# Weight sums of a seven-product FFN moved from VectorE to adding DMA transfers in DRAM

## The chip, the cores and the metric

The kernel runs on one core of a Trainium2 chip. Its engines work from queues of their own and meet through semaphores: TensorE (PE: matmuls; PEld: its weight loads), VectorE (DVE), ScalarE (ACT), GpSimd (POOL) and SyncE (SP). SP only issues DMA transfers here; POOL issues a few and does small elementwise work; 16 DMA engines move the bytes of all queues. The metric is the device time of one execution in microseconds, as the median of several runs. In the profile L12 is line 12 of the kernel's file.

## The reference

One transformer layer on 512 tokens of width 1024, in float32, batch 1:

```
mod = silu(c) @ w_ada + b_ada                    # 9 rows: shift, scale, gate, three times
u = rms_norm(x) * (1 + sc1) + sh1
x = x + 0.5 * g1 * swiglu(u, ffn1_w_in, ffn1_w_out)
z = (rms_norm(x) * (1 + sc2) + sh2) @ w_mix + b_mix
y_a = sigmoid(o) * rms_norm(mlstm(conv(q, k), v, i, f))     # 4 heads
y_b = forgetting_attention(q, k, v, f)                      # 16 heads
x = x + g2 * ((sigmoid(g_a) * (y_a @ w_a) + sigmoid(g_b) * (y_b @ w_b)) @ w_out)
u = rms_norm(x) * (1 + sc3) + sh3
x = x + 0.5 * g3 * swiglu(u, ffn2_w_in, ffn2_w_out)

swiglu(u, w_in, w_out):  a, b = split(u @ w_in);  return (silu(a) * b) @ w_out
```

The hidden width of both FFNs is 2816, which is 22 blocks of 128. The change concerns the last product, h @ ffn2_w_out, with h = silu(a) * b.

## The kernel before, in words

**Precision.** Every float32 operand of a product is split into a high part (a copy rounded to float32r by ScalarE, L89) and a low part (the difference, by VectorE, L91), and each product is three matmuls (L108 to L110). A weight tile of 128 x 1024 arrives through SP into one of three buffers `raw` and is split into one of four pairs `wh`, `wl`; 24 matmuls use it.

**Stages.** In order of time: start and first FFN (to about 395 us of the span), the second norm, q and k with their convolution (to 467), four mLSTM heads whose weights W are built from a bias tile (to 550), 16 attention heads (to about 850), the two branches and the output projection (to about 1000), the third norm, the second FFN's input products (to about 1210), and its output products (to the end).

**The mLSTM heads.** `mlstm_w(h)` loads a row into all partitions (`Mb`, through SP), POOL adds a mask to it (`Mm`, L837), ScalarE takes exponentials of `Mm` and `Mb` into `W` (L850, L852), TensorE forms q k in four banks t, and VectorE multiplies the banks into `W` (L854), which empties them. `Mm`, `Mb` and the head's results share four buffers. The masks are made by POOL just before the first head (L1182, L1183). `fox_t` prepares attention heads in pairs; for the first two pairs POOL clears tiles `klz` (L946). POOL's next work after these is the addition of the two branches (L1253).

**The second FFN's output in seven products.** The 22 blocks of h make 11 pairs, the tokens are taken in two halves of 256 and the columns of ffn2_w_out in two halves of 512. A pair is then a product of 2 x 2 blocks, which is done with seven block products (Winograd's form) in place of eight. That needs sums on both sides:

- of h, in `pair_h`: for the pair's blocks E (even) and Ra (odd), VectorE forms four combinations while the second FFN's input products run (L384 to L389);
- of the weights, in `pair_weights`: with a0, a1 the column halves of the pair's even rows and b0, b1 those of its odd rows, it makes a1-a0, b0-b1+a1-a0, b1-a1+a0 and b1-a1. Each half of a pair's columns is loaded to SBUF by two transfers of 256 KB (L427), summed there by four VectorE operations of 128 x 256 (L434 to L437), and stored to a DRAM tile `ws` of 1 MB per pair by a transfer of 512 KB (L439). It is a generator: `ffn_in` steps it twice per block of h.

`pair_out` loads the sums from `ws` as further weight tiles and adds up the seven products: first P1, X and Y over all pairs, whose combinations U2 and U4 serve both token halves, then four more products, whose banks are added to x with the right signs at the end (`add`, L503 and L505).

**What sets the order.** The program is written as if sequential. A planner lays the instructions onto the engines' queues by its own costs: an instruction may be laid as soon as its operands are ready in the plan, and among ready ones the one written first goes first. On the chip each queue runs strictly in the planned order, and an instruction that waits holds those behind it. `issue_after(i)` ties what is written under it behind instruction i on the same queue, without a wait for i to end. Waits for data are put in by the framework. In the old version the loads of the sums are tied behind the last weight load, and the sums behind the last product of h.

Of the kernel before, what the change touches and what calls it, by code (L numbers as in the profile page):

```python
# [11 lines left out]
F32 = mybir.dt.float32  # L12
# [3 lines left out]
ALU = mybir.AluOpType  # L16
# [30 lines left out]
class Layer:  # L47
# [309 lines left out]

    def pair_h(self, ps_a, ps_b, j, c0, c1, hp, tp):  # L360


        nc = self.nc
        i, w, h0 = j // 2, c1 - c0, c0 // 256
        nh = w // 256
        s = self.tmp(tp, "sl")
        nc.scalar.activation(s[:, :w], ps_a[:, c0:c1], AF.Silu)
        hv = lambda t: t.rearrange("p (h t) -> p h t", t=256)
        if j % 2 == 0:
            if h0 == 0:  # L370
# [12 lines left out]
        A1 = self.A1[i] = hp.tile([P, 6, 256], F32R, name=self.nm("A1"), tag=f"A{i}", bufs=1)  # L383
        V(E[:, 1, :], E[:, 3, :], Ra[:, 1, :], op=ADD)  # L384
        V(E[:, 2, :], E[:, 1, :], E[:, 0, :], op=SUB)
        nc.scalar.activation(A1[:, 0:3, :], E[:, 0:3, :], AF.Copy)
        V(A1[:, 3:6, :], E[:, 0:3, :], A1[:, 0:3, :], op=SUB)
        V(Rb[:, 0, :], E[:, 0, :], E[:, 3, :], op=SUB)
        V(Rb[:, 1, :], Ra[:, 0, :], E[:, 2, :], op=SUB)  # L389

    def pair_rest(self, i, hp, dt):
# [17 lines left out]
            nc.vector.tensor_tensor(lo[n], R, hi, op=SUB)  # L409
        self.A2[i] = A2, *lo  # L410

    def pair_weights(self, w, hp, tp):


        nc = self.nc
        V = nc.vector.tensor_tensor
        NP = NJ // 2
        self.ws = [self.dp.tile([P, 4, 512], F32, name=self.nm("ws")) for i in range(NP)]
        ts = {}
        def load(u):  # L420
            i, c = u // 2, slice(u % 2 * 256, u % 2 * 256 + 256)

            t = ts[u] = hp.tile([P, 5, 256], F32, name=self.nm("s"), tag=f"A{NP - 1}", bufs=1) if u % 2 else                 tp.tile([P, 5, 256], F32, name=self.nm("s"), tag="st", bufs=1)
            for n in range(2):
                r = (2 * i + n) * P
                with self.tc.issue_after(self.last_raw.ins):
                    nc.sync.dma_start(t[:, 2 * n:2 * n + 2, :], w[r:r + P, :].rearrange("p (h n) -> p h n", h=2)[:, :, c])  # L427
        def sums(u):

            t = ts[u]  # L430
            s = lambda n: t[:, n, :]

            with self.tc.issue_after(self.last_mul.ins):
                V(s(4), s(3), s(1), op=SUB)  # L434
                V(s(1), s(1), s(0), op=SUB)
                V(s(3), s(3), s(1), op=SUB)
                V(s(2), s(2), s(3), op=SUB)  # L437
        def store(u):
            nc.sync.dma_start(self.ws[u // 2][:, :, u % 2 * 256:u % 2 * 256 + 256], ts.pop(u)[:, 1:5, :])  # L439
        for h in range(3 * NP + 1):  # L440
            m, r = h // 3, h % 3
            for u, n in ((2 * m, r), (2 * m + 1, r - 1), (2 * m - 1, r + 2)):
                if 0 <= u < 2 * NP and 0 <= n < 3:
                    (load, sums, store)[n](u)
            yield

    def pair_out(self, w, v, hp, tp, x_src):
# [32 lines left out]
        for tb in range(2):  # L480
            nc.scalar.activation(P1[tb], Z[tb], AF.Copy)
        for tb in range(2):
            V(U2[tb], X[tb], P1[tb], op=ADD)
        for tb in range(2):
            V(U4[tb], Y[tb], U2[tb], op=ADD)
        self.pair_split(NP - 1, hp, tp)
# [11 lines left out]
        g = [new("gb") for _ in range(2)]  # L498
        for h in range(2):
            nc.sync.dma_start(g[h], self.mod_d[v:v + 1, h * 512:(h + 1) * 512].to_broadcast([P, 512]))  # L500
        def add(src, half, tbs):
            t = self.tmp(tp, "rs")
            nc.vector.scalar_tensor_tensor(t, src, 0.5, g[half], op0=MUL, op1=MUL)  # L503
            for tb in tbs:
                V(self.x[tb][half], self.x[tb][half], t, op=ADD)  # L505
        def store(tb, half):
            nc.sync.dma_start(self.out[0, tb * P:(tb + 1) * P, half * 512:(half + 1) * 512], self.x[tb][half])
        tail = 2
        for i in range(NP - tail):
            o = prepare(i)  # L510
            for n in ("WZXY" if i == 0 else "ZYXW"):
                for tb in range(2):
                    step(n, tb, i, o)
            if i == 4:
                self.x_tiles()
                x_src()
            if i in (6, 7):
                tb = i - 6
                add(P1[tb], 0, (tb,))
                add(U2[tb], 0, (tb + 2,))  # L520
                add(U4[tb], 1, (tb, tb + 2))
        os = [prepare(i) for i in range(NP - tail, NP)]
        for n in "ZYXW":
            for tb in range(2):
                for i, o in enumerate(os):
                    step(n, tb, NP - tail + i, o)
                ps = banks[n][tb]
                if n == "Z":
                    add(ps, 0, (tb,))
                    store(tb, 0)  # L530
                elif n == "Y":
                    add(ps, 1, (tb,))
                    store(tb, 1)
                elif n == "X":
                    add(ps, 1, (tb + 2,))
                    store(tb + 2, 1)
                    add(ps, 0, (tb + 2,))
                else:
                    add(ps, 0, (tb + 2,))
                    store(tb + 2, 0)  # L540
# [568 lines left out]
    def run(self):  # L1109
# [67 lines left out]
        with tc.tile_pool(name="att", bufs=1) as ip:  # L1177
            self.maskM = ip.tile([P, P], F32, name="maskM")
            self.maskF = ip.tile([P, P], F32, name="maskF")
            for t, fill, sgn in ((self.maskM, BIG, 1), (self.maskF, -BIG, -1)):  # L1180

                nc.gpsimd.memset(t, 0.0)  # L1182
                nc.gpsimd.affine_select(t, t, pattern=[[sgn, P]], compare_op=ALU.is_ge, fill=fill,  # L1183
                                        base=0, channel_multiplier=-sgn)
            self.onz = ip.tile([P, NT, 2], F32, name="onz")
            nc.gpsimd.memset(self.onz[:, :, 0:1], 1.0)
# [19 lines left out]
            for h0, n, fill in ((0, 3, with_gates(self.v_mlstm(1, ip, ip), 1)), (2, 4, with_gates(self.fox_qkv(0, ip), 1))):  # L1206
                for f, h in ((self.mlstm_w, h0), (self.mlstm_w, h0 + 1), (self.mlstm_h, h0), (self.mlstm_h, h0 + 1)):
                    f(h, ip)
                    advance(fill, n)
                    if f == self.mlstm_h and h == 2:  # L1210
                        self.fox_t(0, yp)
                advance(fill, 99)
            for n in range(18):
                if n % 4 == 0 and n < 16:
                    advance(fill, 99)
                    g = n // 4
                    fill = with_gates(self.fox_qkv(g + 1, ip), 4) if g < 3 else (s for m in range(NK) for s in self.y_a(m, yp, ip))
# [56 lines left out]
        with tc.tile_pool(name="f2t", bufs=1) as tp, tc.tile_pool(name="f2h", bufs=1) as hp:  # L1274
# [1 line left out]
                self.dump(f"u3_{k}", self.uh[k].bitcast(F32))  # L1276
            x_spill(1)
            self.ffn_in_halves(A["ffn2_w_in"][0], 2, hp, tp)
            pw = self.pair_weights(A["ffn2_w_out"][0], hp, tp)
            step = lambda *_: next(pw, None)  # L1280
            self.ffn_in(A["ffn2_w_in"][0], 2, hp, tp, step, step)
            for _ in pw:
                pass
            self.pair_out(A["ffn2_w_out"][0], 8, hp, tp, lambda: self.x_load(self.x3_d))


# [28 lines left out]
```

## Time and profile before

| | us |
|---|---|
| median of 3 runs | 1354.39 |
| lowest and highest | 1353.95, 1356.48 |
| the profiled execution | 1354.64 |
| its span, first to last instruction | 1352.9 |
| granted TensorE clock | 0.999 |

The page gives the busy time of each engine as a share of the span, the chain of work that ended last with its shares by engine, and groups of equal instructions (line, engine, operation, written tile <- read tiles, shapes, count, then busy us and mean ns of one, then the idle time of the engine just before them). The timeline lists instructions with start and duration in us, and in brackets the idle time before one and what ended it. A row of a tile's view gives the shortest, median and longest duration in ns and the first and last start. Rows of transfers end with the KB of one and, for POOL's queue, the median us from issue to landing. The lines themselves stand in the prediction, beside the sentences that use them.

### The profile page before, as it was taken

What the parts mean: (1) busy time and instruction counts of PE and PEld (TensorE: products, weight loads), DVE (VectorE), ACT (ScalarE), POOL (GpSimd) and SP (SyncE); (2) the same over time, 40 slices, a digit from 0 to 9 for tenths busy, and PEclk for the clock granted to TensorE, in tenths of its full rate; (3) what the DMA queues carried; (4) which work ended last, traced back from release to release, by engine and by line L of the source; (5) the groups of instructions that cost most, each with busy time, mean ns of one, the idle gap of its engine ahead of it and who ended that gap; (6) DMA issues with size and microseconds to landing.
All of it is one profiled execution on the core that took longest, in us unless ns stands there. A gap on an engine that the chain in (4) does not pass through costs nothing.

```text
span 1352.9 us, 17800 instructions
## 1 busy us (share of the span) xinstructions
PE 1328.6 (98%) x6520; PEld 1113.0 (82%) x6520; DVE 887.8 (66%) x1661; ACT 589.4 (44%) x978; POOL 46.0 (3%) x71
## 2 busy tenths in 40 slices
PE   7999999999999999999999999999999999999997
PEld 6788887887888888988888888888788888888886
DVE  6866666655558767987686876446475655545776
ACT  4532333322235755556565676333353222223642
POOL 2000000000011101000000000002010000000000
PEclk9999999999999999999999999999999999999999
DMA  9676556665634434444243442354436677763474
GB/s 290 187 225 187 179 178 212 218 201 183 200 86 105 129 91 126 116 131 121 74 140 86 113 141 78 110 183 159 140 110 183 212 232 219 228 189 139 171 247 166
DMA packets 245691, 219.30 MB, mean 162 GB/s; under 512 B 12706, under 2 KB 206914, under 8 KB 245604
## 3 DMA queue, kind: packets, MB, share of 16 engines
q1 hardware_dynamic: 245124, 218.09, 52.9%
q8 instruction: 51, 0.84, 0.2%
q14 instruction: 36, 0.29, 0.1%
q0 software_dynamic: 416, 0.06, 0.0%
q10 hardware_dynamic: 64, 0.02, 0.0%
HBM read 194.47 MB, written 23.66 MB: 161 GB/s over the span
## 4 chain that ended last, share of the span: by engine, by line
PE 86%; DVE 7%; ACT 3%; DMA 2%; issue 1%; SPq 0%; DVEq 0%; ACTq 0%
PE g L110 22%; PE g L108 22%; PE g L109 22%; PE t L110 4%; PE t L108 4%; PE t L109 4%; PE g L697 2%; PE t L1041 2%; PE t L1011 1%; DVE wl L91 1%; PE t L982 1%; PE t L983 1%; PE t L697 1%; DVE fq L961 1%; DMA h_d<-hn 1%
## 5 line engine op out<-in xcount | busy, mean ns | idle before, releaser
L89 ACT ACTIVATE wh<-raw 128x1024 fp32r<-128x1024 f32 x236 | 244.2, 1040 | 434.1 <-PE g L109 143.4
L91 DVE TENSOR_TENSOR wl<-raw,wh 128x1024 fp32r<-128x1024 f32 x236 | 290.0, 1231 | 188.2 <-ACT wh L89 168.6
L108 PE MATMUL g<-uh,wh 128*128 128x512 f32 (+2 forms) x984 | 370.6, 377 | 0.8 <-ACT wh L89 0.7
L110 PE MATMUL g<-uh,wl 128*128 128x512 f32 (+2 forms) x984 | 369.6, 376 | 1.0 <-DVE wl L91 1.0
L109 PE MATMUL g<-ul,wh 128*128 128x512 f32 (+2 forms) x984 | 369.6, 376 | 0.0
L110 PEld LDWEIGHTS g<-uh,wl 128*128 128x128 f32 (+1 forms) x984 | 184.7, 188 | 35.7 <-DVE wl L91 1.8
L108 PEld LDWEIGHTS g<-uh,wh 128*128 128x128 f32 (+1 forms) x984 | 184.8, 188 | 34.5 <-ACT wh L89 1.4
L109 PEld LDWEIGHTS g<-ul,wh 128*128 128x128 f32 (+1 forms) x984 | 184.9, 188 | 33.2
L108 PE MATMUL g<-wh,uh 128*128 128x512 f32 (+1 forms) x320 | 111.9, 350 | 0.0
L110 PE MATMUL g<-wh,ul 128*128 128x512 f32 (+1 forms) x320 | 111.1, 347 | 0.0
L109 PE MATMUL g<-wl,uh 128*128 128x512 f32 (+1 forms) x320 | 110.9, 347 | 0.0
L284 DVE SCALAR_TENSOR_TENSOR acc<-raw,ccol,acc 128x1024 f32<-128x1024 f32 x49 | 62.8, 1282 | 13.0 <-DMA raw<-in_w_ada_dram 12.1
L108 PEld LDWEIGHTS g<-wh,uh 128*128 128x128 f32 x320 | 60.5, 189 | 7.8 <-DVE tk L896 0.5
L110 PEld LDWEIGHTS g<-wh,ul 128*128 128x128 f32 x320 | 60.5, 189 | 7.7
L109 PEld LDWEIGHTS g<-wl,uh 128*128 128x128 f32 x320 | 60.5, 189 | 7.4
L108 PE MATMUL g<-yh,wh 128*128 128x512 f32 x128 | 50.4, 394 | 0.0
L110 PE MATMUL g<-yh,wl 128*128 128x512 f32 x128 | 50.2, 392 | 0.0
L109 PE MATMUL g<-yl,wh 128*128 128x512 f32 x128 | 49.7, 388 | 0.0
L993 ACT ACTIVATE S<-S,mn 128x128 f32<-128x128 f32 (+1 forms) x64 | 35.6, 557 | 18.5 <-DVE mn L985 9.5
L108 PE MATMUL g<-wh,hh 128*128 128x512 f32 x88 | 35.0, 398 | 0.0
L110 PE MATMUL g<-wh,hl 128*128 128x512 f32 x88 | 34.9, 396 | 0.0
L108 PE MATMUL t<-wh,hh 128*128 128x512 f32 x88 | 34.8, 396 | 0.0
(319 smaller groups left out, 2054.8 us busy)
## 6 DMA issues: line engine op xcount, KB each, us to landing
raw<-in_ffn_w_in_dram SPq DMA_DIRECT2D x82, 512.0 KB
raw<-in_w_ada_dram SPq DMA_DIRECT2D x56, 512.0 KB
raw<-in_w_mix_dram SPq DMA_DIRECT2D x48, 512.0 KB
raw<-in_ffn_w_out_dram SPq DMA_DIRECT2D x33, 512.0 KB
s<-in_ffn_w_out_dram SPq DMA_DIRECT2D x44, 256.0 KB
ws<-s SPq DMA_DIRECT2D x22, 512.0 KB
ar<-in_w_ada_dram SPq DMA_DIRECT2D x32, 256.0 KB
raw<-in_w_mix_dram SPq DMA_DIRECT2D x32, 256.0 KB
```

The lines of the kernel that those rows point to most:

```text
L89: nc.scalar.activation(hi, src, AF.Copy)
L91: nc.vector.tensor_tensor(lo, src, hi, op=SUB)
L108: mm(ps, lh, rh, start=start, stop=False)
L109: mm(ps, lh, rl, start=False, stop=False)
L110: self.last_mm = mm(ps, ll, rh, start=False, stop=stop)
L284: nc.vector.scalar_tensor_tensor(acc, r, self.ccol[:, k:k + 1], acc, op0=MUL, op1=ADD)
L697: mm = nc.tensor.matmul(acc_ps[b], (wl if p == 1 else wh)[:, b % 2, s], self.ul[k] if p == 2 else self.uh[k], start=k == 0 and p == 0, sto ...
L961: nc.vector.scalar_tensor_tensor(lo, b[own, :], gc[own, :], d[own, :], op0=MUL, op1=SUB)
L982: nc.tensor.matmul(ps[:, :w], q[:, s], k[:, :w], start=True, stop=False)
L983: nc.tensor.matmul(ps[:, :w], q[:, s], kl[:, :w], start=False, stop=True)
L993: nc.scalar.activation(S[:, ws], S[:, ws], AF.Exp, scale=-1.0, bias=m, accum_out=sm[:, qb:qb + 1])
L1041: nc.tensor.matmul(po[:, q0:], vt[:, kb, i, :], Px[:, o:o + T - q0], start=n == 1, stop=n == 8)
```

## The change

The sums of the weights no longer pass through SBUF. For each pair three transfers copy a0, the two halves (b0, b1) and again b1 from ffn2_w_out into `ws`, DRAM to DRAM; four transfers that add to their target then make a0+a1, b1+a1, b0+(the first) and b0+b1+a0+a1. All 77 are issued on POOL's queue, tied behind the second mask's instruction (`mask`); the generator is stepped in the loop over the attention heads, and a pair's copies are written one step ahead of its sums. Since such a transfer only adds, the sums have other signs than before (a0+a1 in place of a1-a0 and so on), and the sums of h, U2 and the last additions to x change sign to match. The loads, VectorE sums and stores beside the second FFN's input products are gone.

```diff
     def pair_h(self, ps_a, ps_b, j, c0, c1, hp, tp):
...
-        V(E[:, 1, :], E[:, 3, :], Ra[:, 1, :], op=ADD)
-        V(E[:, 2, :], E[:, 1, :], E[:, 0, :], op=SUB)
+        V(E[:, 1, :], E[:, 3, :], Ra[:, 1, :], op=SUB)
+        V(E[:, 2, :], E[:, 0, :], E[:, 1, :], op=SUB)
         nc.scalar.activation(A1[:, 0:3, :], E[:, 0:3, :], AF.Copy)
         V(A1[:, 3:6, :], E[:, 0:3, :], A1[:, 0:3, :], op=SUB)
-        V(Rb[:, 0, :], E[:, 0, :], E[:, 3, :], op=SUB)
+        V(Rb[:, 0, :], E[:, 3, :], E[:, 0, :], op=SUB)
         V(Rb[:, 1, :], Ra[:, 0, :], E[:, 2, :], op=SUB)
...
-    def pair_weights(self, w, hp, tp):
...
+    def pair_weights(self, w, anchor):
+
+        G = self.nc.gpsimd
         NP = NJ // 2
         self.ws = [self.dp.tile([P, 4, 512], F32, name=self.nm("ws")) for i in range(NP)]
...
+        row = lambda r: w[r * P:(r + 1) * P, :].rearrange("p (h n) -> p h n", h=2)
+        def copies(i):
+            a, b, t = row(2 * i), row(2 * i + 1), self.ws[i]
+            G.dma_start(t[:, 0, :], a[:, 0, :])
+            G.dma_start(t[:, 1:3, :], b)
+            G.dma_start(t[:, 3, :], b[:, 1, :])
+        with self.tc.issue_after(anchor.ins):
+            copies(0)
+        for i in range(NP):
+            with self.tc.issue_after(anchor.ins):
+                if i + 1 < NP:
+                    copies(i + 1)
+                a, t = row(2 * i), self.ws[i]
+                G.dma_start(t[:, 0, :], a[:, 1, :], accum_op=ADD)
+                G.dma_start(t[:, 3, :], a[:, 1, :], accum_op=ADD)
+                G.dma_start(t[:, 2, :], t[:, 0, :], accum_op=ADD)
+                G.dma_start(t[:, 1, :], t[:, 2, :], accum_op=ADD)
             yield
...
         for tb in range(2):
-            V(U2[tb], X[tb], P1[tb], op=ADD)
+            V(U2[tb], X[tb], P1[tb], op=SUB)
...
-        def add(src, half, tbs):
+        def add(src, half, tbs, op=ADD):
             t = self.tmp(tp, "rs")
             nc.vector.scalar_tensor_tensor(t, src, 0.5, g[half], op0=MUL, op1=MUL)
             for tb in tbs:
-                V(self.x[tb][half], self.x[tb][half], t, op=ADD)
+                V(self.x[tb][half], self.x[tb][half], t, op=op)
...
-                add(U2[tb], 0, (tb + 2,))
+                add(U2[tb], 0, (tb + 2,), SUB)
...
-                    add(ps, 0, (tb + 2,))
+                    add(ps, 0, (tb + 2,), SUB)
...
-                nc.gpsimd.affine_select(t, t, pattern=[[sgn, P]], compare_op=ALU.is_ge, fill=fill,
+                mask = nc.gpsimd.affine_select(t, t, pattern=[[sgn, P]], compare_op=ALU.is_ge, fill=fill,
...
+
+            pw = self.pair_weights(A["ffn2_w_out"][0], mask)
             for n in range(18):
+                next(pw, None)
                 if n % 4 == 0 and n < 16:
...
             self.ffn_in_halves(A["ffn2_w_in"][0], 2, hp, tp)
-            pw = self.pair_weights(A["ffn2_w_out"][0], hp, tp)
-            step = lambda *_: next(pw, None)
-            self.ffn_in(A["ffn2_w_in"][0], 2, hp, tp, step, step)
-            for _ in pw:
-                pass
+            self.ffn_in(A["ffn2_w_in"][0], 2, hp, tp)
             self.pair_out(A["ffn2_w_out"][0], 8, hp, tp, lambda: self.x_load(self.x3_d))
```

More of the change, by code (lines that the diff above doesn't have):

```diff
@@ L410, in pair_split @@
         self.A2[i] = A2, *lo
-    def pair_weights(self, w, hp, tp):
-        nc = self.nc
-        V = nc.vector.tensor_tensor
+    def pair_weights(self, w, anchor):
+        G = self.nc.gpsimd
         NP = NJ // 2
         self.ws = [self.dp.tile([P, 4, 512], F32, name=self.nm("ws")) for i in range(NP)]
[L419 to L444, printed above, removed]
```

## The prediction

> **What bounds the kernel now.** First the page's busy shares, then the chain that ended last.
>
> ```profile
> span 1352.9 us, 17800 instructions
> PE 1328.6 (98%) x6520; PEld 1113.0 (82%) x6520; DVE 887.8 (66%) x1661; ACT 589.4 (44%) x978; POOL 46.0 (3%) x71
> PE 86%; DVE 7%; ACT 3%; DMA 2%; issue 1%; SPq 0%; DVEq 0%; ACTq 0%
> ```
>
> TensorE is busy 98% and carries 86% of the chain; POOL is nearly empty. An average can hide a stage with another limit, so I took the busy time by stretches: the first FFN (100 to 150), the four mLSTM heads (473.8 to 550), the first attention head (550 to 600), the second FFN's input products with the weight sums beside them (1052 to 1204), and the output products just behind, without sums (1204 to 1250). Columns: stretch, busy us and instructions of PE, PEld, DVE, ACT, POOL, then granted clock, DMA share, GB/s.
>
> ```profile
> 100.00:150.00 50.00, 50.00 (x222) 41.16 (x221) 31.54 (x33) 18.21 (x22) 0.00 (x0) 1.00 0.58 177
> 473.80:519.20 45.40, 45.40 (x240) 39.40 (x239) 34.36 (x104) 22.32 (x59) 1.09 (x4) 1.00 0.34 101
> 500.00:550.00 50.00, 50.00 (x282) 44.08 (x282) 40.86 (x130) 26.64 (x68) 3.63 (x4) 1.00 0.40 119
> 550.00:600.00 50.00, 49.43 (x297) 43.72 (x296) 41.56 (x128) 28.06 (x57) 0.00 (x0) 1.00 0.43 116
> 1052.00:1204.00 152.00, 152.00 (x672) 125.88 (x671) 84.10 (x153) 42.14 (x50) 0.00 (x0) 1.00 0.73 223
> 1204.00:1250.00 46.00, 46.00 (x205) 38.09 (x204) 20.55 (x28) 14.43 (x21) 0.00 (x0) 1.00 0.45 147
> ```
>
> A busy PE need not be a PE at its pace, so I divide: 152.00/672 = 0.226 us per matmul with the sums beside it, 46.00/205 = 0.224 without them, 50.00/222 = 0.225 in the first FFN, which never had any. The rate is the same at a DMA share of 0.73 and of 0.45 and with VectorE at 55% or 45%. In the stage from which work is taken, TensorE alone sets the pace.
>
> **What is removed.** Grouped by the tile s, and by transfer:
>
> ```profile
> L427 SPq DMA_DIRECT2D s<-in_ffn_w_out_dram x44: 539/602/823, 1002.7 to 1195.6; - x44
> L434 DVE TENSOR_TENSOR s<-s x22: 414/418/428, 1035.2 to 1201.6; 128x256 f32<-128x256 f32 x22
> L439 SPq DMA_DIRECT2D ws<-s x22: 562/567/588, 1037.6 to 1204.4; - x22
> 1035.00:1205.00 170.00, 35.27 (x88) 1.00 0.73 220
> s<-in_ffn_w_out_dram SPq DMA_DIRECT2D x44, 256.0 KB
> ws<-s SPq DMA_DIRECT2D x22, 512.0 KB
> ```
>
> That is 88 VectorE sums, 35.27 us in 170; 44 loads and 22 stores, 23 MB together; and on SP's queue 44 × 0.602 + 22 × 0.567 = 39 us of issuing. All of it runs under TensorE's unbroken stream, so I cost the removal at **0 us**. It would be worth up to 35 us only if TensorE waited for VectorE there, and the 0.226 beside 0.224 excludes more than 672 × 0.002 = 1.3 us.
>
> **The signs.** Per pair one VectorE addition becomes a subtraction and two subtractions swap operands; at the first combination the two U2 sums become differences, and four of the last additions to x subtractions. None is added.
>
> ```profile
> L384 DVE TENSOR_TENSOR E<-E,Ra 128x256 f32<-128x256 f32 x11 | 4.6, 421 | 0.1
> L385 DVE TENSOR_TENSOR E<-E 128x256 f32<-128x256 f32 x11 | 4.6, 421 | 0.1
> ```
>
> L384 adds and L385 subtracts, both at 421 ns: **0 us**, before the end and in the tail.
>
> **What is added, and where it lands.** 77 transfers on POOL's queue: per pair three copies (256, 512, 256 KB) and four adding transfers of 256 KB, so 1.05 MB of copies and 1.05 MB of sums, 11 times. They are written inside the loop over the 16 heads, but their only ties are the queue order behind the last mask instruction and the data order among themselves. POOL's timeline shows what the planner does with such work:
>
> ```profile
> 467.26 0.29 POOL L1183 TENSOR_SCALAR_AFFINE_SELECT maskF<-maskF 128x128 f32<-128x128 f32 x1
> 467.54 0.10 POOL L1187 MEMSET onz<- 128x4 f32 x1
> 471.29 2.54 POOL L837 TENSOR_TENSOR Mm<-Mb,maskM 128x512 f32<-128x512 f32 x2 [3.66 <-DMA Mb<-M_d]
> 481.10 1.09 POOL L946 MEMSET klz<- 64x512 f32 x2 [7.26 <-issue]
> 519.19 1.30 POOL L837 TENSOR_TENSOR Mm<-Mb,maskM 128x512 f32<-128x512 f32 x1 [37.00 <-DVE rq L135]
> 526.28 1.29 POOL L837 TENSOR_TENSOR Mm<-Mb,maskM 128x512 f32<-128x512 f32 x1 [5.80 <-DMA Mb<-M_d]
> 527.63 1.09 POOL L946 MEMSET klz<- 64x512 f32 x2
> 912.68 2.33 POOL L1253 TENSOR_TENSOR sg<-sg,ta 128x512 f32<-128x512 f32 x1 [383.96 <-DMA raw<-in_w_branch_b_dram]
> ```
>
> The first klz memsets are written behind the whole third mLSTM head, yet they ran at 481.10, before that head's Mm at 519.19: work without inputs is laid into POOL's earliest gap. So the copies begin at 467.6, not at the heads, and fill the 45.4 us between the second and the third Mm (473.83 to 519.19). Behind them in the same queue stand Mm of heads 2 and 3 and one klz pair, then nothing until 912.68.
>
> What does a queued transfer cost POOL? Its own early transfers tell:
>
> ```profile
> 2.35 0.54 POOL L152 DMA_DIRECT2D rowsA<-in_ffn_norm_g_dram  x1
> 2.88 0.54 POOL L152 DMA_DIRECT2D rowsA<-in_conv_w_dram  x1
> 3.41 0.54 POOL L152 DMA_DIRECT2D rowsA<-in_conv_b_dram  x1
> ...
> 7.14 0.52 POOL L152 DMA_DIRECT2D rowsA<-in_b_mix_dram  x1 [0.64 <-DMA rowsA<-in_ffn_norm_g_dram]
> 9.34 0.52 POOL L166 DMA_DIRECT2D gbias<-in_b_mix_dram  x1 [0.67 <-DMA rowsA<-in_conv_b_dram]
> rowsA<-in_b_mix_dram POOLq DMA_DIRECT2D x2, 4.0 KB, 6.1
> rowsA<-in_mix_norm_g_dram POOLq DMA_DIRECT2D x1, 4.0 KB, 3.3
> ```
>
> 0.54 us to issue a small one, 3.3 to 6.1 us to land. Counted in the timeline's order, the tenth transfer (7.14) waited for the landing of the second (2.35), the twelfth (9.34) for that of the fourth (3.41): eight are in flight at most, and POOL stands still meanwhile.
>
> Three unknowns follow, each bounded from rows.
>
> Pace on the chip, per pair. In the gap the engines are 0.34 busy at 101 GB/s, so 297 GB/s when full and 196 spare. Copies: 1.05 MB/196 = 5.4 us. Sums: 5.4 if they cost what a copy does, 10.7 if reading the target doubles it. A pair takes 10.7 to 16.1 us; I take 13.4, the middle. The data order asks for about the same: copy, first sum, second sum land one after another, three landings of 3.3 to 6.1 us, 10 to 18.
>
> The Trainium skill (DMA: Bandwidth & Descriptors, "Anatomy of one DMA — SWDGE (gpsimd) path") fits a POOL transfer as 2.0 us plus bytes over 436 GB/s, 2.6 us for 256 KB. The trace differs: 4 KB alone took 3.3 to 6.1 us. By the fit, an estimate, three landings would make 7.8 us a pair and the third Mm would not be late; I go by the rows.
>
> Pace in the plan. At least 7 × 0.54 = 3.8 us a pair, at most three landings at the short end, 9.9. I take 9.0, near the upper end, since the sums must wait for landings in the plan too. Then 45.4/9.0 = 5.04 pairs, 35 transfers, stand ahead of the third Mm. None at all would be the bound below.
>
> Cover. What waits for Mm, and how long it can:
>
> ```profile
> 520.52 0.70 ACT L850 ACTIVATE W<-Mm,gcol 128x128 f32<-128x128 f32 x2 [0.42 <-POOL Mm L837]
> 522.40 1.04 ACT L89 ACTIVATE wh<-raw 128x1024 fp32r<-128x1024 f32 x1
> 521.34 1.67 DVE L854 SCALAR_TENSOR_TENSOR W<-t,W 128x512 f32<-128x512 f32 x4
> 530.16 0.39 PE L108 MATMUL t<-qkh,qkh 128*128 128x512 f32 x1
> 534.16 0.28 DVE L854 SCALAR_TENSOR_TENSOR W<-t,W 128x128 f32<-128x128 f32 x1
> 543.00 0.28 PE L108 MATMUL t<-vm,Wh 128*128 128x258 f32 x1
> ```
>
> ScalarE's exponential L850 waits for Mm, and behind it in ScalarE's order stands the next weight split (522.40); behind VectorE's L854, which empties the four t banks by 523.01, stand the low halves. TensorE needs those banks at 530.16: **7.15 us** of cover. For the fourth head, banks are empty at 534.44 and needed at 543.00: 8.6 us.
>
> **The sum.** 5.04 × 13.4 = 67.6 us for 45.4: the third Mm is 22.2 us late, TensorE stands 22.2 − 7.15 = 15.0 us. Between the third and fourth Mm lie 7.09 us in the plan, 0.79 pairs, 10.6 us on the chip: 10.6 − 8.6 = 2.0 more. TensorE has no slack later to win it back. 0 + 0 + 15.0 + 2.0 = 17.0 us. The profiled execution took 1354.64 us (its span 1352.9, 1.7 around it), 0.25 above the median 1354.39; 1354.6 + 17.0 = 1371.6, in round numbers **1371 us**. With 10.7 us a pair the third Mm is 8.5 late, the sum 1.4, 1356; with 16.1 the sum is 32.7, 1387. With 16.1 and a plan of 8.0 a pair (5.68 pairs) it is 46.0 − 7.15 + 14.3 − 8.6 = 44.6, 1399. With all 11 pairs ahead of Mm, 11 × 13.4 − 45.4 − 7.15 = 95, 1450.
>
> **Rivals.**
>
> *Covered: no change.* If a pair lands in under (45.4 + 7.15)/5.04 = 10.4 us, or the plan keeps most pairs behind the fourth Mm, nothing reaches TensorE. For it: 10.7, the low bound, is close to 10.4, and no POOL work follows before 912.68. Against: the eight-in-flight wait is POOL's own standstill, and the plan ranks nothing above a ready transfer while Mm's input is missing. 1354.6 us.
>
> *The loads get too little.* Weight loads want 119 GB/s (500 to 550). If they get a third of 297 GB/s while sums run, 99, they lack 17% over 11 × 13.4 = 147 us: 25 us without cover, 0 with the full lead of three raw and four split tiles (24 matmuls of 0.225 us each, 38 us). I take 5: 1360 us. It decides from 119 GB/s down.
>
> *POOL's issue is held up by VectorE.* VectorE is busy 40.86 of 50 us with 130 instructions, 0.31 us each. If each issue waits for one, a pair takes 7 × 0.31 = 2.2 us more, 15.6: third Mm 33.2 late, 26.1 + (12.3 − 8.6) = 29.8, 1384 us. The Trainium skill (SBUF — State Buffer, "Who interferes with whom") has a VectorE operation in a two-port mode hold the port that POOL needs to write descriptors. No row here shows it, since POOL issued its transfers in the first 11 us alone.
>
> *The sums are far slower.* Above (912.68 − 467.3)/11 = 40.5 us a pair they would also hold the branch additions; the third Mm alone would be 159 late, over 1500 us.
>
> *Slightly faster* could come only from a reshuffled order in the heads, where 550 to 600 has 50 − 49.43 = 0.57 us of idle TensorE, at that rate 3.8 us up to 880; I see no mechanism. 1351 us.
>
> **How the numbers follow.** Forecast 50% (1356 to 1399), covered 28%, loads 9%, issue 6%, far slower 4%, reshuffled 3%. No change means within 0.2%, 2.7 us, about what a measurement of this kernel can tell. Faster 5%: the reshuffle and the lucky edge of covered. Same 29%: covered and the forecast's lower edge. Slower 66%. The range must take in 1354.6 with its spread and the forecast with its upper doubts: 1351.5 to 1400, leaving out the far slower case, the plan with all pairs ahead, and the larger reshuffles. The forecast's own range is 1356 to 1399.
>
> **What would show it.** Right: 77 transfers start near 467.6; the third Mm runs near 541 instead of 519.19, released by a transfer; the matmul stream breaks between 530 and 550, and 1052 to 1204 keeps 0.226 us per matmul. Wrong: Mm at 519 with transfers behind it (covered); a whole stream but raw loads releasing L89 in the heads (loads); a second FFN with matmuls closer than 0.224 us, which would break the argument that nothing is gained there.

## The result, and the profile after

| | before | after |
|---|---|---|
| median of 4 runs, us | 1354.83 | 1412.47 |
| lowest and highest | 1353.95, 1356.48 | 1411.12, 1416.03 |
| ratio, 95% interval | | 1.0427 (1.0414 to 1.044) |
| profiled execution, its span | 1354.64, 1352.9 | 1416.03, 1414.2 |

The change costs 57.6 us. The page of the changed kernel: the busy shares, the granted clock in 40 slices of 35 us (in tenths, 9 is 90% or more), POOL's DMA queue (packets, MB, share of 16 engines) and its groups of transfers (KB each, median us from issue to landing).

```profile
PE 1341.9 (95%) x6520; PEld 1122.5 (79%) x6520; DVE 859.7 (61%) x1573; ACT 588.9 (42%) x978; POOL 100.2 (7%) x148
PEclk9999999999999995899999999999999999999999
q0 software_dynamic: 10096, 23.13, 7.9%
ws<-in_ffn_w_out_dram POOLq DMA_DIRECT2D x44, 256.0 KB, 8.6
```

TensorE has the same 6520 matmuls and a share of 95 in place of 98%. The clock drops in two slices, the sixteenth and seventeenth: 530 to 601 us, the mLSTM heads. A transfer of 256 KB from the weights lands after 8.6 us. Busy time by stretches, columns as in the prediction (the view's DMA shares can come out a little above 1):

```profile
473.80:519.20 45.40, 45.40 (x237) 39.18 (x236) 31.82 (x90) 22.23 (x58) 19.47 (x28) 1.00 1.02 246
519.20:550.00 30.80, 15.53 (x58) 12.03 (x56) 3.79 (x19) 2.21 (x8) 10.37 (x15) 0.75 0.99 212
550.00:600.00 50.00, 27.79 (x166) 25.35 (x167) 21.20 (x54) 16.84 (x38) 20.68 (x29) 0.75 0.90 194
600.00:650.00 50.00, 42.35 (x212) 35.83 (x211) 33.35 (x115) 20.12 (x44) 8.44 (x11) 0.93 0.78 187
1100.00:1150.00 50.00, 50.00 (x222) 41.42 (x221) 19.77 (x26) 14.30 (x17) 0.00 (x0) 1.00 0.32 95
```

Up to 519 TensorE hardly notices that the DMA share has gone from 0.34 to 1.02 (237 matmuls in place of 240). From there to 650 it idles 15.27 + 22.21 + 7.65 = 45 us. In the second FFN the pace is 50.00/222 = 0.225 us per matmul, as before, though the DMA share there fell to 0.32: the removal frees an engine and the transfers, and TensorE has no use for either. POOL's timeline in the stretch between (most transfers left out):

```profile
468.34 0.29 POOL L1173 TENSOR_SCALAR_AFFINE_SELECT maskF<-maskF 128x128 f32<-128x128 f32 x1
468.65 0.56 POOL L421 DMA_DIRECT2D ws<-in_ffn_w_out_dram  x1
...
475.71 1.30 POOL L827 TENSOR_TENSOR Mm<-Mb,maskM 128x512 f32<-128x512 f32 x1
...
568.32 1.55 POOL L827 TENSOR_TENSOR Mm<-Mb,maskM 128x512 f32<-128x512 f32 x1
...
579.41 1.59 POOL L827 TENSOR_TENSOR Mm<-Mb,maskM 128x512 f32<-128x512 f32 x1
...
625.00 1.09 POOL L936 MEMSET klz<- 64x512 f32 x2
```

The transfers start right behind the mask; 6 stand ahead of the second Mm, 53 ahead of the third, 60 ahead of the fourth, all 77 ahead of the last klz. The third Mm runs at 568.32 (before: 519.19). What TensorE waited for, from the timelines of SP, ScalarE and TensorE:

```profile
520.99 0.33 SPq L824 DMA_DIRECT2D Mb<-M_d  x1
534.04 0.61 ACT L842 ACTIVATE W<-Mb,gcol 128x384 f32<-128x384 f32 x1 [13.30 <-DMA Mb<-M_d]
535.28 0.80 PE L108 MATMUL g<-wh,uh 128*128 128x512 f32 x1 [10.32 <-ACT tg L1069]
535.87 0.63 PE L109 MATMUL g<-wl,uh 128*128 128x512 f32 x1
536.30 0.63 PE L110 MATMUL g<-wh,ul 128*128 128x512 f32 x1
...
541.55 0.39 PE L108 MATMUL g<-wh,uh 128*128 128x512 f32 x1
541.79 0.39 PE L109 MATMUL g<-wl,uh 128*128 128x512 f32 x1
...
569.90 0.69 ACT L840 ACTIVATE W<-Mm,gcol 128x128 f32<-128x128 f32 x2 [34.67 <-POOL Mm L827]
571.08 0.79 PE L108 MATMUL t<-qkh,qkh 128*128 128x512 f32 x1 [25.94 <-DVE W L844]
```

The same load and its reader before the change:

```profile
513.59 0.38 SPq L834 DMA_DIRECT2D Mb<-M_d  x1
518.90 0.62 ACT L852 ACTIVATE W<-Mb,gcol 128x384 f32<-128x384 f32 x1 [1.93 <-DMA Mb<-M_d]
```

Three things are to be read here. First, the row Mb, a transfer on SP's queue that has nothing to do with POOL's, reaches its reader 13.05 us after its issue (534.04 − 520.99; before 5.31). ScalarE stands at L842, with tg behind it, and TensorE stands 10.32 us. The row is also issued 7.4 us later than before (520.99, 513.59), and transfers had a part in that too, as a row of ScalarE and SP's waits show (us in total, times, longest):

```profile
503.68 1.06 ACT L89 ACTIVATE wh<-raw 128x1024 fp32r<-128x1024 f32 x1 [7.54 <-DMA raw<-in_w_mix_dram]
SPq L824 <- DMA h_d<-hn: 3.5, 2, 3.3
SPq L961 <- DMA h_d<-hn: 10.4, 2, 6.8
```

A weight split stood 7.54 us for its load (before, the split at this place, 499.44, waited for TensorE), VectorE's work on hn came late behind it, and SP then stood 3.5 us until hn's stores to DRAM, which free the buffer that Mb takes, had landed. The later row A (L961) was held up in the same way, once for 6.8 us (before, once for 2.9). Second, Mm, which is behind 53 transfers, holds it for another 25.94 us. Third, after each stop 512 columns take 0.43 us from start to start in place of 0.23, for some 5 us (535.28 to 540.57 after the first).

### The profile page after: what moved, and what is told of

Its sections match the earlier page's. It is cut to its first block, busy times and chain, and to the rows that moved or that the text cites. A ratio compares the mean times of both kernels' runs of the same rounds, so it can differ in the third digit from the quotient of the medians.

```text
span 1414.2 us, 17703 instructions
## 1 busy us (share of the span) xinstructions
PE 1341.9 (95%) x6520; PEld 1122.5 (79%) x6520; DVE 859.7 (61%) x1573; ACT 588.9 (42%) x978; POOL 100.2 (7%) x148
## 5 line engine op out<-in xcount | busy, mean ns | idle before, releaser
L89 ACT ACTIVATE wh<-raw 128x1024 fp32r<-128x1024 f32 x236 | 244.1, 1039 | 430.5 <-PE g L109 144.1
L108 PE MATMUL g<-wh,uh 128*128 128x512 f32 (+1 forms) x320 | 114.4, 357 | 13.5 <-ACT tg L1069 10.3
L247 POOL TENSOR_TENSOR ul<-uf,uh 128x256 fp32r<-128x256 f32 x16 | 13.4, 838 | 450.2 <-DVE uf L246 450.2
L1246 POOL TENSOR_TENSOR sg<-sg,ta 128x512 f32<-128x512 f32 x8 | 11.4, 1424 | 374.6 <-DMA raw<-in_w_branch_b_dram 346.4
L844 DVE SCALAR_TENSOR_TENSOR W<-t,W 128x512 f32<-128x512 f32 (+3 forms) x16 | 7.2, 487 | 47.3 <-ACT W L840 46.2
```

What stands on the lines that cost most here:

```text
L89: nc.scalar.activation(hi, src, AF.Copy)
L108: mm(ps, lh, rh, start=start, stop=False)
L247: (nc.gpsimd if k % 2 else nc.vector).tensor_tensor(self.ul[k][:, c0:c0 + w], uf[:, :w], self.uh[k][:, c0:c0 + w], op=SUB)
L844: nc.vector.scalar_tensor_tensor(W[:, ws], ps[:, c0:], float(P) ** -0.5, W[:, ws], op0=MUL, op1=MUL)
L1246: nc.gpsimd.tensor_tensor(t, t, ta[m], op=ADD)
```

## The experiments

Times are medians; "above" is the difference from the median of before taken in the same session (1354.33 to 1355.75). The theory at the start: the 57.6 us come from POOL's queue order, that is from Mm behind the transfers. The rival: the transfers slow other traffic.

### e1_no_transfers: only the removal and the signs

```diff
-        self.ws = [self.dp.tile([P, 4, 512], F32, name=self.nm("ws")) for i in range(NP)]
+        self.ws = [w[2 * i * P:(2 * i + 2) * P, :].rearrange("(p two) (h n) -> p (two h) n", two=2, h=2) for i in range(NP)]
...
-            copies(0)
...
+        yield
```

> Weight sums left out: the output products read the plain weight rows where they read the sums, so neither the old sums nor the new transfers are there; the signs are those of the changed kernel. Theory (the whole loss is made by the 77 transfers, and the removal and the signs are worth nothing because TensorE alone sets the pace beside the old sums): 1353 to 1357 us. Rival (the removal frees something, which the loss hides): under 1350. Rival (the signs or the new order of the other engines cost): over 1360.

1357.86 us, 2.1 above, ratio 1.0016 (1.0006 to 1.0027). Neither the freed 35 us of VectorE nor the freed transfers bring anything, and the other signs cost nothing that could be 57 us. The 2 us are not theirs either: e5 below, which has the removal, the signs and the true sums, has none.

### e2_vector: the queue order undone

```diff
-        nc.gpsimd.tensor_tensor(b4(Mm), b4(Mb), self.maskM[:, None, :].to_broadcast([P, NT, P]), op=ADD)
+        nc.vector.tensor_tensor(b4(Mm), b4(Mb), self.maskM[:, None, :].to_broadcast([P, NT, P]), op=ADD)
...
-                nc.gpsimd.memset(self.klz[p][h][64 - h * 64:P - h * 64, :].bitcast(F32), 0.0)
+                nc.vector.memset(self.klz[p][h][64 - h * 64:P - h * 64, :].bitcast(F32), 0.0)
```

> The four mask additions and the klz memsets go to VectorE; the 77 transfers stay as they are, so nothing of the heads stands behind them in POOL's queue. Theory (queue order: the third mask addition behind 53 transfers makes the 26 us stall, a slower landing of its input the 10 us stall before it): the 26 us and the slow clock after it go, the landing stays: 1365 to 1385. Rival (the DMA engines are overrun and every load is late, queue order or not): 1400 to 1415.

1395.39 us, 39.6 above (1.0295, 1.0272 to 1.0318): between the two expectations. With nothing but transfers in POOL's queue, only 18 of the 57.6 us are gone. The timelines show what took Mm's place:

```profile
519.29 0.33 SPq L824 DMA_DIRECT2D Mb<-M_d  x1
535.51 0.69 DVE L827 TENSOR_TENSOR Mm<-Mb,maskM 128x512 f32<-128x512 f32 x1 [15.34 <-DMA Mb<-M_d]
536.75 0.79 PE L108 MATMUL g<-wh,uh 128*128 128x512 f32 x1 [12.96 <-ACT tg L1069]
...
623.19 1.97 PE L944 MATMUL t<-ident,tk 128*128 128x128 f32 x8 [9.98 <-DVE mn L975]
```

Mb lands 16 us after its issue. It is needed as soon as it can be there, so its landing time goes straight to TensorE.

### e8_vector_alone: the control of e2

```diff
# e1_no_transfers, and in it
-        nc.gpsimd.tensor_tensor(b4(Mm), b4(Mb), ...
+        nc.vector.tensor_tensor(b4(Mm), b4(Mb), ...
-                nc.gpsimd.memset(self.klz[p][h][64 - h * 64:P - h * 64, :].bitcast(F32), 0.0)
+                nc.vector.memset(self.klz[p][h][64 - h * 64:P - h * 64, :].bitcast(F32), 0.0)
```

> The control of the run e2_vector: no transfers (weight sums left out, the output products read plain rows), Mm and klz on VectorE. Theory (what e2_vector lost, 40 us, is contention on the DMA engines): 1353 to 1360 us. Rival (the additional VectorE work in the heads itself stalls TensorE): 1365 us or more.

1357.02 us, 2.1 above (1.0016, 1.0007 to 1.0026), as e1. VectorE can carry Mm and klz; what e2 lost comes from the transfers.

### e3_behind_klz: all transfers behind POOL's work of the heads

```diff
-                nc.gpsimd.memset(self.klz[p][h][64 - h * 64:P - h * 64, :].bitcast(F32), 0.0)
+                self.klz_last = nc.gpsimd.memset(self.klz[p][h][64 - h * 64:P - h * 64, :].bitcast(F32), 0.0)
...
-            pw = self.pair_weights(A["ffn2_w_out"][0], mask)
...
-                next(pw, None)
+                if n == 2:
+                    pw = self.pair_weights(A["ffn2_w_out"][0], self.klz_last)
+                if n >= 2:
+                    next(pw, None)
```

> The 77 transfers are tied behind the last klz memset, the last work of the heads in POOL's queue, in place of the mask; the generator starts two heads later. Theory (queue order): no POOL work waits, what is left is slower landings beside the attention heads: 1355 to 1366. Rival (overrun DMA engines): the same 23 MB beside loads of the same rate, 1380 or more.

1388.5 us, 32.8 above (1.0258, 1.0215 to 1.0301). The rival held, against the theory: Mm comes 3.5 us later than before, TensorE does not stop for it, and most of the loss is still there, at another place.

```profile
522.70 1.29 POOL L827 TENSOR_TENSOR Mm<-Mb,maskM 128x512 f32<-128x512 f32 x1 [37.48 <-DVE hn L874]
...
569.02 0.33 SPq L961 DMA_DIRECT2D A<-A_d  x1
582.10 0.69 DVE L964 TENSOR_TENSOR Am<-A,maskF 128x512 f32<-128x512 f32 x1 [9.15 <-DMA A<-A_d]
607.96 1.97 PE L944 MATMUL t<-ident,tk 128*128 128x128 f32 x8 [11.97 <-DVE mn L975]
```

Now it is A, the row that the first attention head takes, with 13.08 us from issue to reader. Before the change that pair of rows is 6.69 us apart:

```profile
561.19 0.45 SPq L971 DMA_DIRECT2D A<-A_d  x1
567.88 0.68 DVE L974 TENSOR_TENSOR Am<-A,maskF 128x512 f32<-128x512 f32 x1
```

From here on the theory has two parts: (a) the queue order, and (b) transfers that are issued just ahead of their use land late while POOL's run.

### e4_copies: what an adding transfer costs

```diff
-                G.dma_start(t[:, 0, :], a[:, 1, :], accum_op=ADD)
-                G.dma_start(t[:, 3, :], a[:, 1, :], accum_op=ADD)
-                G.dma_start(t[:, 2, :], t[:, 0, :], accum_op=ADD)
-                G.dma_start(t[:, 1, :], t[:, 2, :], accum_op=ADD)
+                G.dma_start(t[:, 0, :], a[:, 1, :])
+                G.dma_start(t[:, 3, :], a[:, 1, :])
+                G.dma_start(t[:, 2, :], t[:, 0, :])
+                G.dma_start(t[:, 1, :], t[:, 2, :])
```

> The weight sums are left out: the 44 adding transfers become plain copies of the same bytes, in the same order and with the same waits. If an adding transfer costs twice a copy, a pair takes about 11 us in place of 14.3, the third mask addition comes some 24 us sooner, 1385 to 1392. If it costs what a copy does, and the waits for landings set the pace, 1405 to 1415.

1387.63 us, 31.9 above (1.0235, 1.0213 to 1.0258). The same bytes, as plain copies in the same order, take less of the DMA engines:

```profile
q0 software_dynamic: 7280, 23.13, 5.7%
```

5.7% of 16 × 1389.6 us is 1267 engine-us for 88 units of 256 KB (eight a pair), 14.4 each. After: 7.9% of 16 × 1414.2 is 1788; less 44 × 14.4 for the copies leaves 1154 for 44 sums, 26.2 each. If a copy takes as long there as here, an adding transfer holds the engines 1.8 times as long as a copy. The queue's pace gains less than that: here the third Mm runs at 551.78, behind 53 transfers that begin at 467.56, which is 11.1 us a pair in place of 13.2.

### e5_ffn2: the same transfers where only prefetched loads run

```diff
-        (nc.gpsimd if k % 2 else nc.vector).tensor_tensor(
+        self.last_ulk = (nc.gpsimd if k % 2 else nc.vector).tensor_tensor(
...
-            pw = self.pair_weights(A["ffn2_w_out"][0], mask)
...
-                next(pw, None)
...
-            self.ffn_in(A["ffn2_w_in"][0], 2, hp, tp)
+            pw = self.pair_weights(A["ffn2_w_out"][0], self.last_ulk)
+            self.ffn_in(A["ffn2_w_in"][0], 2, hp, tp, lambda j: next(pw, None))
```

> All 77 transfers as in the changed kernel, but tied behind the last POOL instruction of the third norm and written beside the second FFN's input products. What is loaded there are prefetched weights only; no row broadcast and no Mm stands behind the transfers. Theory (they cost time only by Mm in POOL's queue and by loads that are issued late and sit on the chain, Mb and A): 1353 to 1359 us, TensorE at 0.225 us per matmul between 1052 and 1204 although the transfers share the DMA engines. Rival (their bytes slow every load that runs beside them, weights too, or the sums of the last pairs are not there when the output products ask for them): 1375 us or more, with weight loads or ws loads releasing TensorE.

1355.21 us, 0.3 above (0.9999, 0.999 to 1.0009): the whole change for nothing. The transfers run from 1014.13 to the last issue at 1165.30, 13.7 us a pair, and in that stretch the windows show:

```profile
1012.00:1170.00 158.00, 158.00 (x741) 132.56 (x740) 65.47 (x87) 44.34 (x53) 56.01 (x79) 1.00 1.04 243
```

The DMA engines are as full as in the heads (1.04, 243 GB/s) and TensorE does not miss a matmul. Full DMA engines cost nothing where every load has a lead.

### e6_two and e10_vector_two: two in flight in place of eight

```diff
+        sent = []
+        def D(*a, **k):
+            i = G.dma_start(*a, **k)
+            if len(sent) > 1:
+                self.tc.add_manual_dep(i.ins, sent[-2].ins.name, mybir.DependencyInfo(
+                    mybir.DependencyClass.Sync, mybir.DependencyReason.DATA), reason="two in flight")
+            sent.append(i)
...
-            G.dma_start(t[:, 0, :], a[:, 0, :])
+            D(t[:, 0, :], a[:, 0, :])
...
```

All seven transfers of a pair go through D. e6 has this beside the edit of e3, e10 beside the edit of e2.

> The transfers tied behind the last klz memset as in the run e3_behind_klz (1388.5 us, 33 above before), with one thing more: each waits until the transfer two before it has landed, so that at most two are in flight in place of eight. Theory (a row broadcast lands late because it queues behind the backlog of POOL's transfers on the DMA engines): the wait of Am for A falls from 13 us to 4 to 7 us, and the time to 1358 to 1372 us. Rival (the bytes count, however many transfers are in flight): A's wait stays over 10 us, 1383 us or more.

> As e2_vector (1395.4 us), with at most two of POOL's transfers in flight in place of eight, each waiting for the transfer two before it; the row broadcasts are where they were. Theory (the backlog of eight makes a row land in 13 us; two leave it at 4 to 7): Mb and A no longer end gaps of over 4 us, 1358 to 1372 us. Rival (bytes count, not the number in flight): the gaps at 523 and 613 stay within 3 us of their 13.1 and 10.1, 1388 us or more.

e6: 1364.44 us, 9.5 above (1.0074, 1.0057 to 1.0091; e3 32.8). e10: 1366.08 us, 11.7 above (1.0085, 1.007 to 1.01; e2 39.6). Both times are in the theory's range. First A of e6, then Mb of e10:

```profile
560.76 0.33 SPq L968 DMA_DIRECT2D A<-A_d  x1
569.37 0.69 DVE L971 TENSOR_TENSOR Am<-A,maskF 128x512 f32<-128x512 f32 x1 [2.52 <-DMA A<-A_d]
```

```profile
516.17 0.33 SPq L831 DMA_DIRECT2D Mb<-M_d  x1
522.61 0.69 DVE L834 TENSOR_TENSOR Mm<-Mb,maskM 128x512 f32<-128x512 f32 x1 [4.19 <-DMA Mb<-M_d]
```

From issue to reader A takes 8.6 us (e3: 13.1), more than the 4 to 7 that the theory gave, and Mb 6.4 (e2: 16.2). The transfers also run slower: e10's last one is issued at 724.01, some 23 us a pair in place of 14. So these two runs do not tell the number in flight from the bytes per us; that stays open.

### e7_small_rows: the queue order without the bytes

```diff
...
-            a, b, t = row(2 * i), row(2 * i + 1), self.ws[i]
-            G.dma_start(t[:, 0, :], a[:, 0, :])
-            G.dma_start(t[:, 1:3, :], b)
-            G.dma_start(t[:, 3, :], b[:, 1, :])
+            a, b, t = row(2 * i), row(2 * i + 1), sums[i]
+            G.dma_start(t[:, 0, :32], a[:, 0, :32])
+            G.dma_start(t[:, 1:3, :32], b[:, :, :32])
+            G.dma_start(t[:, 3, :32], b[:, 1, :32])
...
-                G.dma_start(t[:, 0, :], a[:, 1, :], accum_op=ADD)
+                G.dma_start(t[:, 0, :32], a[:, 1, :32], accum_op=ADD)
...
```

The small transfers fill tiles `sums` that nobody reads; the output products read the plain weight rows, as in e1.

> 77 transfers on POOL's queue at the changed kernel's place, each of 32 columns in place of 512, so a sixteenth of the bytes (16 or 32 KB). The weight sums are left out: the output products read plain rows of ffn2_w_out. The plan keeps the third Mm behind about as many transfers as in the changed kernel. If the pace of the queue comes from the bytes (8.6 us for 256 KB against a few us for 16 KB), 53 transfers take under 53 x 0.9 = 48 us, the third Mm starts before 525 and the time is 1354 to 1362 us. If it comes from issue and landing, which do not shrink with the bytes (seven transfers in 14.2 us, the sums one behind another), Mm comes after 545 and the time is 1370 us or more.

1367.99 us, 13.1 above (1.0095, 1.008 to 1.011): neither case. The premise was off: the planner put all 77 ahead of the third Mm, so it seems to price transfers by their bytes too. But the rows separate the terms:

```profile
469.06 0.57 POOL L422 DMA_DIRECT2D ws<-in_ffn_w_out_dram  x1
...
502.58 1.67 POOL L433 DMA_DIRECT2D ws<-in_ffn_w_out_dram  x1
503.12 1.67 POOL L422 DMA_DIRECT2D ws<-in_ffn_w_out_dram  x1
...
534.73 1.66 POOL L828 TENSOR_TENSOR Mm<-Mb,maskM 128x512 f32<-128x512 f32 x1
```

77 transfers in 534.73 − 469.06 = 65.7 us are 0.85 us each, 6.0 us a pair. In the changed kernel 53 take 568.32 − 468.65 = 99.7 us, 1.88 each, 13.2 a pair. More than half of the pace is bytes; at 0.85 the 53 would have been through at 514, ahead of Mm's time. What the late Mm costs here, 15.5 us late and with 1.5 MB in place of 23 beside it, is at most 13.1 − 2.1 (e1) = 11 us.

The stop itself shows the clock, apart from any load on the DMA engines (TensorE's timeline, then a window behind the stop):

```profile
537.60 0.73 PE L108 MATMUL t<-qkh,qkh 128*128 128x512 f32 x1 [4.19 <-DVE W L845]
538.13 0.63 PE L109 MATMUL t<-qkl,qkh 128*128 128x512 f32 x1
538.56 0.63 PE L110 MATMUL t<-qkh,qkl 128*128 128x512 f32 x1
...
537.50:542.00 4.50, 4.40 (x16) 3.98 (x17) 3.85 (x9) 3.79 (x10) 0.37 (x1) 0.62 0.33 66
```

After 4.19 us of idling, 512 columns start 0.43 us apart at a DMA share of 0.33: the half rate follows the stop, not the transfers.

### e9_vector_early_rows and its control e11_rows_alone: rows loaded early

```diff
# e9: e2_vector, e11: e8_vector_alone, and in both
-        Mb = ip.tile([P, T], F32, name=self.nm("Mb"), tag="bc", bufs=4)
+        Mb = ip.tile([P, T], F32, name=self.nm("Mb"), tag="rows", bufs=2)
...
-        Mm = ip.tile([P, T], F32, name=self.nm("Mm"), tag="bc", bufs=4)
+        Mm = ip.tile([P, T], F32, name=self.nm("Mm"), tag="bc", bufs=2)
# A0 as Mb; hn and Am as Mm
```

> As e2_vector (transfers at the mask, Mm and klz on VectorE; 1395.4 us), with one thing more: the row broadcasts Mb and A get two buffers of their own, and Mm, hn and Am share two, in place of four for all. Nothing is computed otherwise. In SP's queue Mb of heads 2 and 3 and the first two A then stand ten places earlier, so they can be loaded long before they are needed. Theory (the contention costs time where a row is loaded just ahead of its use): the 13.1 us gap of TensorE at 523 goes, the 10.1 us gap at 613 goes or shrinks below 4, with the half-rate stretches behind them; 1360 to 1378 us. Rival (it is the transfers' bytes, whatever waits for them, so the weight loads become the next wait): a gap of over 8 us stays in 520 to 640 and the time is 1388 us or more.

> The control of e9_vector_early_rows (1388.9 us): the same buffers and the same order, without the transfers (weight sums left out, the output products read plain rows). In e9 the Mm of head 2 waited 12.1 us for hn's store to DRAM, since Mm and hn share two buffers. Theory (that store, too, lands late because of the transfers' backlog, so the next transfer on the chain took the place of Mb): 1355 to 1362 us, and the wait of Mm for h_d under 6 us. Rival (two buffers are too few whatever runs beside them): 1375 us or more, with the wait for h_d over 8 us.

e9: 1388.93 us, 34.6 above (1.0248, 1.0231 to 1.0265), a miss for the theory as I had put it. The time is the rival's (1388 or more), but its gap of over 8 us is not there (the longest is 7.08). Mb and A no longer end large gaps, but only 5 us came of it. The third Mm now waits for the buffer it takes over from hn, and that is free when hn's store to DRAM has landed. What VectorE waited for ahead of Mm, in e9 and then in e11, which has the same buffers and no transfers (us, times):

```profile
  DMA h_d<-hn: 12.1, 1
```

```profile
  DMA h_d<-hn: 4.3, 1
```

e11 takes 1356.7 us, 1.8 above (1.0016, 1.0007 to 1.0026): the two buffers are enough when the store lands in time. So part (b) holds in a wider form: it is not the two rows alone but transfers with no lead, stores that free a buffer included; here one row got a lead and the next such transfer took its place.

### e12_five_pairs: the prediction's own number of transfers ahead of Mm

```diff
+            if i == 5:
+                anchor = self.klz_last
             with self.tc.issue_after(anchor.ins):
-                if i + 1 < NP:
+                if i == 5:
+                    copies(i)
+                if i + 1 < NP and i != 4:
                     copies(i + 1)
...
-                next(pw, None)
+                if n == 0:
+                    pw = self.pair_weights(A["ffn2_w_out"][0], mask)
+                    advance(pw, 5)
+                if n >= 2:
+                    next(pw, None)
```

> The changed kernel with the number of transfers ahead of the third Mm made to be what the prediction took: five pairs (35 transfers) at the mask, the other six (42 transfers) tied behind the last klz memset; all else as in the changed kernel. If the count (53 in place of 35) was the prediction's only fault, its sum holds here: third Mm 536 to 546, one stall of about 15 us, 1366 to 1378 us. Theory (a second term is missing: while transfers run, rows and stores that are issued just ahead of their use land late, which cost 33 us in e3_behind_klz after the klz memsets alone): third Mm in the same place, and gaps of TensorE behind 560 as well, 1390 to 1408 us.

1399.7 us, 45.4 above (1.0336, 1.0317 to 1.0355). Here 35 transfers stand ahead of the third Mm, as the prediction had it:

```profile
531.14 0.61 ACT L846 ACTIVATE W<-Mb,gcol 128x384 f32<-128x384 f32 x1 [13.61 <-DMA Mb<-M_d]
532.38 0.79 PE L108 MATMUL g<-wh,uh 128*128 128x512 f32 x1 [9.10 <-ACT tg L1073]
537.09 1.58 POOL L831 TENSOR_TENSOR Mm<-Mb,maskM 128x512 f32<-128x512 f32 x1
...
622.89 1.97 PE L948 MATMUL t<-ident,tk 128*128 128x128 f32 x8 [10.90 <-DVE mn L979]
```

Mm runs at 537.09 (the prediction: near 541), and yet the time is 28 us over the forecast. TensorE's first stop ends on Mb before Mm is even due, and its second long one, at 623, is the wait for A.

## Why the prediction was wrong

**Removal and signs at nothing: right.** e1 and e5, and 0.225 us per matmul in the second FFN.

**Start behind the mask, in POOL's order: right**, 468.65.

**13.4 us a pair on the chip: right.** 13.2 ahead of the third Mm, 14.2 over all 77 (625.00 − 468.65 over 11). In part this is luck. By e4 the sums hold the engines 1.8 times as long as copies, where I took 1.5; with its 11.1 us for seven copies my working would then give 11.1 × (1 + 1.8)/2 = 15.5, and the queue took 13.2. The Trainium skill's fit (DMA: Bandwidth & Descriptors, "Anatomy of one DMA — SWDGE (gpsimd) path") of 2.6 us for 256 KB is not borne out under this load: 8.6 us.

**9.0 us a pair in the plan: the first step that failed.** Between the second and the third Mm the planner laid 53 − 6 = 47 transfers, where I had put 35: 45.4 us over 6.7 pairs, 6.8 us a pair if the plan's gap is the 45.4 us measured before. I had bounds of 3.8 and 9.9 and went close to the upper one, arguing that the plan must wait for landings; it waits less than that. With the third Mm as late as it was, 568.32 − 519.19 = 49.1 us, the prediction's own sum is 49.1 − 7.15 = 42.0 for it and 579.41 − 568.32 − 8.6 = 2.5 for the fourth, 44.5, so 1399. That is still 13 short of the 1412, and e12 shows why the count is not the main fault.

**The transfers' effect on other traffic, at nothing in the sum and at 5 us in a rival of 9%: the term that was mis-sized most.** I priced it by the weight loads' rate, 119 GB/s, and by their lead. Weight loads had a small part: the sign that I had named, a load that releases L89 late in the heads, is there once (503.68), but no stop of TensorE over 2 us in the changed kernel ends on one directly. What I left out were transfers without a lead: the rows Mb and A, which the heads ask for right behind their issue, and hn's stores, which hold up the issue of these rows. With the queue order undone they cost 39.6 us (e2), behind the heads' POOL work 32.8 (e3); with the transfers in flight cut to two, 9.5 to 11.7. The warning stood in rows that I had quoted: the first and the fourth Mm of before wait 3.66 and 5.80 us for Mb. A transfer that is waited for at a DMA share of 0.4 was waited for longer at 1.0.

**Cover of 7.15 us: right for Mm, and beside the point.** In e7 Mm is 15.5 us late; TensorE reaches the banks 533.41 − 530.16 = 3.25 us later than before and then waits 4.19 us, which leaves 8.1 us of cover. I followed what waits for Mm, L850 of ScalarE. The first instruction on the tile W is L852, which waits for Mb alone and holds the same queue. It stopped TensorE for 10.3 us, before Mm was missed.

**Left out: the clock.** After a stop TensorE runs at half rate for some 5 us; the two large stops of the changed kernel cost 12 × 0.2 = 2.4 us and about 2 us more than their length. In all, TensorE's idle time grew by 48.0 us (72.3 beside 24.3 of the two spans) and its busy time for the same matmuls by 13.3 (1341.9 beside 1328.6). Two smaller stops of 4.28 and 2.71 us (before 613.93 and 653.93) have the half clock behind them too; how the rest of the 13.3 divides was not worked out.

**The terms do not add.** Mm behind 53 transfers is worth 18 us beside e2, and behind 35 (e12) only some 45.4 − 39.6 = 6 (roughly, since e12 also issues its last 42 later), as Mb holds up the same place at the same time. That the forecast's 17 us and the 18 us by which e2 undercuts the changed kernel are so close is an accident.

**Issue held up by VectorE: not seen.** In e7 POOL issued 0.54 us apart (502.58, 503.12) in the heads, where VectorE is busy three quarters of the time (33.71 of 45.4 us); the rule that I cited for it (the Trainium skill, SBUF — State Buffer, "Who interferes with whom") decides nothing here.

No version was found that beats the kernel before; e5 equals it, with VectorE and SP relieved where TensorE sets the pace.

## What to carry to other kernels

Ask of added background transfers not how much bandwidth is left but which transfers beside them have no lead: a row that is used as soon as it lands, a store that frees a buffer. Where there are none, a full DMA system cost nothing (e5, 0.3 us); where there are some, the same bytes cost 33 to 40 us, and allowing only two in flight, which also slowed the transfers, gave back some 70% of it. Instructions that a planner may lay into an idle queue go where the queue is idle, ahead of whatever is written earlier but is not ready yet: count them there, from the planned order.

## What the runs showed of the hardware

- **Half clock after a stop.** After 4.19 us of idling (e7) the next matmuls of 512 columns start 0.43 us apart in place of 0.23, at a granted clock of 0.62 over the 4.5 us behind it. The Trainium skill (TensorE: Matmul & The Clock Gate, "Why this matters for your kernels") says to leave no gap of over about 3 us between matmul bursts, or the clock goes back to half. The traces agree for the longer gaps: every stop of TensorE of 3 us or more between 400 and 1300 us in these runs has the half rate behind it within 2 us. Shorter ones go either way, and the measurement decides: one of 1.98 us in the changed kernel has it (matmul at 650.45, granted 0.51 from 650.4 to 651.3), one of 2.37 us in e3 has not (568.15, granted 1.00 for 2 us behind it), nor one of 1.67 us in e10 (258 columns 0.12 us apart right behind it).
- **An adding transfer in DRAM holds the engines 1.8 times as long as a copy** (26.2 and 14.4 engine-us for 256 KB, by the queues' shares of packet time), yet seven transfers took 13.2 us with four adding ones and 11.1 with none.
- **One queue's transfers delay another's.** A row of 2 KB for 128 partitions on SP's queue, 5.3 to 6.7 us from issue to reader before, took 13 to 16 us beside POOL's transfers with up to eight in flight (some four on average, an estimate: they land after about 8.3 us and 77 take 156), and 6.4 to 8.6 with at most two, which came at 23 us a pair in place of 14.
- **A POOL transfer has a price without bytes**: 0.85 us each in a row of 77 with a sixteenth of the bytes, waits for landings included, in place of 1.88.
